# A hybrid attention and HGRN layer on one core: attention tails through one copy, six shared tiles for down sums, and the last channel's additions behind the meta rows

## The chip, the cores and the metric

The kernel runs on one core of a Trainium2 chip. The metric is the device time of one execution in microseconds. A core has TensorE (PE, matmuls; PEld is its weight load), VectorE (DVE), ScalarE (ACT), GpSimd (POOL) and SyncE (SP), which here issues the DMAs. Each engine runs its own queue in order and waits on semaphores of the others. Matmuls write PSUM, which has banks of 128 partitions by 512 float32; ACT and DVE read it.

## The reference

One layer over 16 meta rows and 1024 tokens (1040 rows, width 1024):

```python
a = rmsnorm(h, ln_mix_pre)
dq, dk, dv, hq, hf, hi, hg = split(a @ w_in)
y_diff = diff_attention(dq, dk, dv, ...)     # 4 heads, softmax minus lam * softmax, then rmsnorm
y_hgrn = hgrn2(hq, hf, hi, hg, ...)          # 4 heads, gated linear recurrence, rmsnorm * silu(g)
mix = concatenate([y_diff, y_hgrn]) @ w_out
h = h + rmsnorm(mix, ln_mix_post)
a = rmsnorm(h, ln_ffn_pre)
u = causal_conv3(a @ w_ffn_up) + conv_b      # 2 * 2816 channels
h = h + rmsnorm((gelu(gate) * up) @ w_ffn_down, ln_ffn_post)
return h[:, 16:, :]
```

All of it is float32. Products are made of three matmuls each: an operand is split into a rounded part `hi` and a remainder `lo`, and hi·hi, hi·lo and lo·hi are added.

## The kernel before, in words

The rows are taken in nine blocks: block 0 holds the meta rows (of which two are needed after the mixing), blocks 1 to 8 the 128-row blocks of tokens. The work on TensorE runs in four stretches:

- up to about 540 us, for each head the projections (`dense`), into which `interleave` puts the steps of attention (`attn`) and of the recurrence (`hgrn_head`) at set distances;
- 540 to 604 us, the first half of the output projection (`out_first`: columns 0 to 511, the first seven of eight channels of 128, into `y0`), with `hgrn_head` of head 3 between;
- 604 to 690 us, the second half, a loop over the blocks: matmuls into `py`, then `post` (norm, residual, norm, giving `a2`, in the profile `a`) and, some blocks later, `trans` (transposes of `a2`, copied to `at2`). The eighth channel comes last, since hgrn head 3 gives it: `out_last` adds it to `y0` from a bank `pz`, with the weight kept from the first half, and chunk 7 of block 1 waits for it likewise;
- then the up-projection with its convolution to about 1110 us, and the down-projection.

TensorE runs in the order in which the code is written. The other engines are ordered by the framework's scheduler, save where `issue_after` or `keep_in_program_order` hold an instruction back, and each engine's queue is then fixed. Tiles come from pools with a given number of buffers; who takes a buffer waits until its last reader is done.

In PSUM there are two banks with tag "ip" (projections, `py` of the first half, `pz`), two with tag "m" (`ss`, `pn`, `pt`, `pa`, `pl`) and two double ones with tag "S" (scores, `py` of the second half).

The tail of a piece of attention (`normed` with no gate; in a profile `ona`, `ss`, `msa`): the normed rows `on` are transposed into a bank `ss`; ACT multiplies the bank by the gain into the rounded `hi`, and DVE reads the bank again for the remainder `lo`. `to_nat` (`pn_vh`: values of the recurrence, transposed) takes the next "m" bank.

`down_sums` makes differences of down weights in spare time of stage one: four `wd` tiles are loaded, DVE subtracts, SP stores. `load_wo(n)` loads the eight output weights of half n through three raw tiles (`wor`) and splits them (`woh`, `wol`); `prep_plain` splits four up weights (`ra` into `uh`, `ul`). `halve` are POOL products over the forget gates in `hgrn_head`.

In the profile L53 is the wrapper through which most ACT and DVE instructions are issued, L146 the POOL subtraction of `split`, L336 the transposes of `to_nat`, L439 those products of `hgrn_head` that are called `pl`, L936 to L940 the three matmuls of `out_part`, and L1122 the transposes of `trans`.

Of the kernel before, what the change touches and what calls it, by code (L numbers as in the profile page):

```python
# [9 lines left out]
F32 = mybir.dt.float32  # L10
# [7 lines left out]
P = 128  # L18
# [4 lines left out]
KD = D // P  # L23
# [62 lines left out]
def layer_kernel(ctx: ExitStack, tc: tile.TileContext, x, meta, table, lbl, gpre, gpost, win,  # L86
# [54 lines left out]
    def ps_s(name):  # L141
        return pp.tile([P, 2, 512], F32, tag="S", name=name)

    def split(hi, lo, raw, eng=None):
        A.copy(hi, raw)
        (eng or G).tensor_tensor(lo, raw, hi.bitcast(F32), op=ALU.subtract)  # L146
# [21 lines left out]
    def parts_store(k, b0, b1, m, off):  # L168
        n = b1 - b0
        for l in range(2):  # L170
            SY.dma_start(msc[b0:b1, :, l, P * k:P * k + P].rearrange("b p c -> p b c"),
                         m[:, l, off:off + P * n].bitcast(F32).rearrange("p (b c) -> p b c", c=P))

    at_cm, atp = pool("at", 1)
    ahi = atp.tile([P, KD, L], F32R, tag="ahi", name="ahi")
    alo = atp.tile([P, KD, L], F32R, tag="alo", name="alo")
    ws_cm, wsp = pool("wdsums", 4)

    last_load = []

# [165 lines left out]

    late = []
    carry = []

    def carried():  # L350
        tails = list(carry)
# [40 lines left out]
    def hgrn_head(t, done=None):  # L392
# [9 lines left out]

        def halve(src, dst):
            pr = src.rearrange("p (b two) -> p b two", two=2)
            G.tensor_tensor(dst, pr[:, :, 0], pr[:, :, 1], op=ALU.mult)

        halve(f, t1)
        halve(t1, t2)
# [131 lines left out]
    def normed(k, b0, src, on, ss, C, n, gain, nm, raw=None, gate=None):  # L540
        if gate is None:
            V.scalar_tensor_tensor(ss[:C, :n], ss[:C, :n], 1.0 / 128, ss[:C, 4:4 + n], ALU.mult, ALU.add)
            A.activation(ss[:C, :n], ss[:C, :n], AF.Ln)
            A.activation(ss[:C, :n], ss[:C, :n], AF.Exp, scale=-0.5)
        else:
            rstd_of(ss[:C, :n], ss[:C, :n], 128.0)
        V.tensor_tensor(on[:C, :n], src, ss[:C, :n].rearrange("p (n o) -> p n o", o=1).to_broadcast([C, n, P]), op=ALU.mult)
        yield 1
        pt = ps_m(f"ss{nm}")
        W = start(b0 + n - 1) + rows(b0 + n - 1) - start(b0)  # L550
        for c in range(n):
            o = max(W - (n - c) * C, 0)
            T.transpose(pt[:, o:o + C], on[:C, c], ident[:C, :C])
        if gate is not None:
            V.scalar_tensor_tensor(raw, pt[:, :W], gain, gate, ALU.mult, ALU.mult)

        def halves(hi, lo, cols):
            if gate is None:
                A.mul(hi, pt[:, cols], gain)
                V.scalar_tensor_tensor(lo, pt[:, cols], gain, hi.bitcast(F32), ALU.mult, ALU.subtract)  # L560
            else:
                A.copy(hi, raw[:, cols])
                V.tensor_tensor(lo, raw[:, cols], hi.bitcast(F32), op=ALU.subtract)

        if b0 == 0:
            halves(m0[:, 0, k], m0[:, 1, k], slice(META - 2, META))
        first = max(b0, 1)
        if b0 + n > first:
            w = P * (b0 + n - first)
            m = parts_tile(nm)  # L570
            halves(m[:, 0, :w], m[:, 1, :w], slice(W - w, W))
            parts_store(k, first, b0 + n, m, 0)
        yield 1
# [327 lines left out]
            t_a, tiles_a = attn_in(h + 1)  # L901
            interleave(dense(tiles_a, None, wd_sums), [hgrn_head(t_h)] + carried(), FH, 1500)

    close(ws_cm, at_cm)
    wo_cm, wop = pool("wo", 10)
    y_cm, yp = pool("y0", 1)
    ml_cm, mlp = pool("mixload", 1)
    y0 = yp.tile([P, NBLK, 512], F32, tag="y0", name="y0")
    ssy = yp.tile([P, NBLK, 4], F32, tag="ssy", name="ssy")
    gpo0 = yp.tile([P, 512], F32, tag="gpo0", name="gpo0")  # L910
    SY.dma_start(gpo0, gpost[:, :512].to_broadcast([P, 512]))

    def load_wo(n):
        res = []
        for k in range(KD):
            raw = wp.tile([P, 512], F32, tag="wr", name=f"wor{n}_{k}", bufs=3)
            last_load.append(SY.dma_start(raw, wout[P * k: P * (k + 1), 512 * n: 512 * (n + 1)]))
# [49 lines left out]
    first_load(2)  # L967
    wo0 = load_wo(0)
    wo0_loaded = last_load[-1]

    def y0_gain(p):
        r = tok(p)[0]
# [2 lines left out]
    def out_last(p):  # L975
        r = tok(p)[0]
        py = ps_in(f"pz{p}")
        m = m0[:, :, KD - 1:] if p == 0 else m7[:, p - 1:p].rearrange("p b l t -> p l b t")
# [56 lines left out]
    def prep(q):  # L1035
        ft, j = divmod(q, 7)
        if ft >= NF or q in made:
            return
        if j == 0:
            load_raw4(ft)  # L1040
            src = raws["11"]
            w_sum("1", raws["21"], raws["22"], ALU.add)
        elif j == 1:
            src = w_sum("2", sums["1"], raws["11"], ALU.subtract)
        elif j == 2:
            src = sums["1"]
# [12 lines left out]
        made[q] = (hi, lo)  # L1059
# [3 lines left out]
    def prep_plain():  # L1063
        load_raw4(0)
        for j, nm in enumerate(("11", "12", "21", "22")):
            where = swp if j % 2 else wp
            hi = where.tile([P, 512], F32R, tag="wh", name=f"uh{nm}", bufs=4)
            lo = where.tile([P, 512], F32R, tag="wl", name=f"ul{nm}", bufs=4)
            split(hi, lo, raws[nm], G)
            plain[nm] = (hi, lo)  # L1070

    m7 = ep.tile([P, 8, 2, P], F32R, tag="e1", name="m7")
    for i in range(1, NBLK):
        SY.dma_start(m7[:, i - 1].bitcast(F32), msc[i][:, :, P * (KD - 1):])
    prep_plain()
    prep(7)
    wo = load_wo(1)
    gpo = qp.tile([P, 512], F32, tag="gpo", name="gpo", bufs=1)
    SY.dma_start(gpo, gpost[:, 512:].to_broadcast([P, 512]))
    gfb = qp.tile([P, D], F32, tag="gfb", name="gfb", bufs=1)  # L1080
# [78 lines left out]
        V.tensor_tensor(b21, b21, b22, op=ALU.subtract)  # L1159
        t_split(p, 5, b21, *last)  # L1160

    for i in (1, 0, 2, 3, 4, 5, 6, 7, 8):
        py = ps_s(f"py1_{i}")
        if i >= 3:
            y0_gain(i)
        if i == 0:
            for _ in out_part(m0, py[:, 0], wo, range(KD), True, True):
                pass
            post(i, py)
            continue  # L1170
        py = py[:, 0]
        m = blocks[i]
        if i + 1 < NBLK:
            second_load(i + 1)
        for _ in out_part(m, py, wo, range(4), True, False):
            pass
        if i == 3:
            trans(1)
            trans(0)
        if i > 3:  # L1180
            trans(i - 2)
        for _ in out_part(m, py, wo, range(4, 7 if i == 1 else 8), False, i > 1):
            pass
        if i == 1:
            for p in range(3):
                out_last(p)
            for _ in out_part(m7[:, 0:1].rearrange("p b l t -> p l b t"), py, wo[KD - 1:], range(1), False, True):
                pass
# [7 lines left out]
        if i < 4:  # L1196
            for p in (1 + 2 * i, 2 + 2 * i):
                out_last(p)
    close(q_cm, ml_cm, y_cm, wo_cm)

    xu_cm, xup = pool("xu", 2)
    t_cm, tp = pool("tsplit", 1)
# [365 lines left out]
```

## Time and profile before

| | us |
|---|---|
| median of 3 timed runs | 1354.03 (1353.2 to 1354.85) |
| profiled execution | 1361.32 |
| its span | 1359.5 |
| TensorE busy | 1296.5 |
| VectorE busy | 914.2 |
| ScalarE busy | 685.4 |
| GpSimd busy | 425.5 |

The mean granted clock of TensorE is 0.992. The span is what the profile covers, and the profiled execution is longer than the timed ones. In the rows of a timeline the first two numbers are start and duration in us, then engine, line, operation, what is written and read, and in brackets how long the engine had been idle before and who released it.

### The profile page before, as it was taken

The numbers are of one execution on the slowest core, as the hardware profiler recorded it, in microseconds if no ns is written. First come the engines' busy times: TensorE is split into PE (matmuls) and PEld (weight loads), VectorE is DVE, ScalarE is ACT, GpSimd is POOL, SyncE is SP. The second block draws the span as 40 slices with busy tenths as digits, with TensorE's granted clock in tenths as the row PEclk, the third lists the DMA queues.
The fourth block names the chain that finished last, engine by engine and source line by source line (L and its number), as shares of the span: only waits on it lengthen the run. The fifth ranks groups of instructions, "written<-read, shape, count | busy, mean of one in ns | idle before, by whom it ended". The sixth has DMA issues, their size and how long they took to land.

```text
span 1359.5 us, 26142 instructions
## 1 busy us (share of the span) xinstructions
PE 1296.5 (95%) x10170; PEld 1192.4 (88%) x10170; DVE 914.2 (67%) x1535; ACT 685.4 (50%) x1615; POOL 425.5 (31%) x334
## 2 busy tenths in 40 slices
PE   6999999999999998998998999999999999999997
PEld 5898989889989997675898999999999998888875
DVE  7666647564746464535698867877877776697586
ACT  6365346535644565335674444544554453554454
POOL 3211211021102110315127566566666641010021
PEclk9999999999999999998999999999999999999999
DMA  6332334243411221765612322223222225965363
GB/s 212 112 125 71 114 107 150 63 138 102 139 47 45 86 71 47 260 192 211 225 43 90 96 76 79 86 75 107 93 70 83 82 78 174 340 200 163 93 201 116
DMA packets 99570, 165.26 MB, mean 122 GB/s; under 512 B 10051, under 2 KB 34915, under 8 KB 99446
## 3 DMA queue, kind: packets, MB, share of 16 engines
q1 hardware_dynamic: 99446, 163.58, 36.6%
q8 instruction: 80, 1.31, 0.4%
q14 instruction: 44, 0.36, 0.1%
HBM read 122.91 MB, written 40.63 MB: 120 GB/s over the span
## 4 chain that ended last, share of the span: by engine, by line
PE 70%; DVE 11%; DMA 7%; ACT 6%; issue 4%; POOL 2%; SPq 1%; DVEq 0%; ACTq 0%; POOLq 0%
PE pd L1414 5%; PE pd L1415 5%; PE pd L1413 5%; PE pb L1255 4%; PE pb L1256 4%; PE pb L1257 4%; DMA wd<-in_wdown_dram 3%; PE pc L1255 2%; PE pa L1255 2%; PE pc L1257 2%; PE pa L1257 2%; PE pa L1256 2%; PE pc L1256 2%; PE pa L708 2%; DVE ast L53 2%
## 5 line engine op out<-in xcount | busy, mean ns | idle before, releaser
L1255 PE MATMUL pb<-t,uh 128*128 128x258 f32 x504 | 143.8, 285 | 5.8 <-DVE u L53 5.7
L1256 PE MATMUL pb<-t,uh 128*128 128x258 f32 x504 | 142.6, 283 | 0.0
L1257 PE MATMUL pb<-t,ul 128*128 128x258 f32 x504 | 142.3, 282 | 0.0
L1414 PE MATMUL pd<-wl,gh 128*128 128x512 f32 x308 | 121.9, 396 | 0.1
L1413 PE MATMUL pd<-wh,gh 128*128 128x512 f32 x308 | 121.7, 395 | 0.0
L1415 PE MATMUL pd<-wh,gl 128*128 128x512 f32 x308 | 121.7, 395 | 0.0
L53 DVE SCALAR_TENSOR_TENSOR c<-uu,cwt,c 128x514 f32<-128x514 f32 (+1 forms) x88 | 96.8, 1100 | 20.6 <-ACT c L53 19.9
L1255 PEld LDWEIGHTS pb<-t,uh 128*128 128x128 f32 x504 | 96.1, 191 | 7.1 <-DVE u L53 7.0
L1222 POOL TENSOR_TENSOR c<-c,c 128x514 f32<-128x514 f32 (+1 forms) x44 | 63.4, 1441 | 121.9 <-ACT c L53 119.2
L1256 PEld LDWEIGHTS pb<-t,uh 128*128 128x128 f32 x504 | 96.1, 191 | 0.0
L1257 PEld LDWEIGHTS pb<-t,ul 128*128 128x128 f32 x504 | 95.9, 190 | 0.0
L1255 PE MATMUL pa<-t,uh 128*128 128x258 f32 (+1 forms) x336 | 95.3, 283 | 0.0
L1256 PE MATMUL pa<-t,uh 128*128 128x258 f32 (+1 forms) x336 | 95.1, 283 | 0.0
L1257 PE MATMUL pa<-t,ul 128*128 128x258 f32 (+1 forms) x336 | 95.0, 283 | 0.0
L1255 PE MATMUL pc<-t,uh 128*128 128x258 f32 (+1 forms) x336 | 94.0, 280 | 0.0
L1257 PE MATMUL pc<-t,ul 128*128 128x258 f32 (+1 forms) x336 | 93.9, 280 | 0.0
L1256 PE MATMUL pc<-t,uh 128*128 128x258 f32 (+1 forms) x336 | 93.7, 279 | 0.0
L53 DVE SCALAR_TENSOR_TENSOR c<-ug,cwt,c 128x514 f32<-128x514 f32 (+1 forms) x88 | 86.0, 977 | 2.7 <-ACT c L53 2.0
L146 POOL TENSOR_TENSOR ul<-ws,uh 128x512 fp32r<-128x512 f32 x42 | 61.4, 1463 | 42.8 <-ACT uh L53 38.2
L1414 PEld LDWEIGHTS pd<-wl,gh 128*128 128x128 f32 x308 | 57.7, 187 | 15.1 <-DVE wl L53 0.9
L53 ACT ACTIVATE pb<-S,ast 128x528 f32<-128x528 f32 (+7 forms) x72 | 46.6, 649 | 47.1 <-DVE ast L53 47.0
L1413 PEld LDWEIGHTS pd<-wh,gh 128*128 128x128 f32 x308 | 57.7, 187 | 14.1
(348 smaller groups left out, 4144.7 us busy)
## 6 DMA issues: line engine op xcount, KB each, us to landing
ra<-in_wup_dram SPq DMA_DIRECT2D x88, 256.0 KB, 2.7
mp<-msc SPq DMA_DIRECT2D x23, 512.0 KB, 5.5
wd<-in_wdown_dram SPq DMA_DIRECT2D x44, 256.0 KB, 4.3
tsc<-wd SPq DMA_DIRECT2D x44, 256.0 KB, 2.6
wi<-tsc SPq DMA_DIRECT2D x44, 256.0 KB, 2.8
gi<-gsc SPq DMA_DIRECT2D x33, 256.0 KB, 4.5
wi<-in_wdown_dram SPq DMA_DIRECT2D x33, 256.0 KB, 2.9
gsc<-c SPq DMA_DIRECT2D x22, 257.0 KB, 2.2
```

The source lines that it names most:

```text
L53: ins = call(*args, **kw)
L146: (eng or G).tensor_tensor(lo, raw, hi.bitcast(F32), op=ALU.subtract)
L708: T.matmul(po[:, :P], w_, vn[:, j], start=(j == 0), stop=(j == i))
L1222: G.tensor_tensor(cg, cg, cu, op=ALU.mult)
L1255: T.matmul(pt, hi[:, s], th[:, k], start=(first and k == 0), stop=False, skip_group_check=True)
L1256: T.matmul(pt, hi[:, s], tl[:, k], start=False, stop=False, skip_group_check=True)
L1257: T.matmul(pt, lo[:, s], th[:, k], start=False, stop=(k == 3), skip_group_check=True)
L1413: T.matmul(py, gh[:, s], wh, start=(k == 0 and pr not in (3, 7)), stop=False, skip_group_check=True)
L1414: T.matmul(py, gh[:, s], wl, start=False, stop=False, skip_group_check=True)
L1415: T.matmul(py, gl[:, s], wh, start=False, stop=(k == NH - 1), skip_group_check=True)
```

## The change

1. Tails of attention: ACT's multiplication by the gain goes into `on` in SBUF and is the only read of the bank. Then ACT casts `hi` from there and DVE subtracts `lo` from there: one ACT instruction more for each piece, as many on DVE.
2. The pool of `wd` tiles has six instead of four, and stays open to the end of the second half. Its tiles then hold output weights 2, 3 and 4 of the first half and 6 and 7 of the second; the pool `wo` shrinks from ten to seven.
3. The POOL subtractions of the four plain up weights and of the second half's even output weights are issued after the last `halve` of hgrn head 3.
4. `gpo0` is loaded after the output weights; the plain up weights and the second half's output weights are called for ahead of the loads of channel 8 (`m7`).
5. In the second half the meta rows are taken inside block 1's turn, ahead of the last channel; `post(1)`, `post(0)` and `out_last(3)`, `out_last(4)` follow. `trans(0)` moves from block 3's turn to block 4's.

```diff
-    def split(hi, lo, raw, eng=None):
+    def split(hi, lo, raw, eng=None, after=None):
         A.copy(hi, raw)
-        (eng or G).tensor_tensor(lo, raw, hi.bitcast(F32), op=ALU.subtract)
+        with nullcontext() if after is None else tc.issue_after(after.ins):
+            (eng or G).tensor_tensor(lo, raw, hi.bitcast(F32), op=ALU.subtract)
...
+    ws_cm, wsp = pool("wdsums", 6)
     at_cm, atp = pool("at", 1)
...
-    ws_cm, wsp = pool("wdsums", 4)
...
-        if gate is not None:
+        if gate is None:
+            raw = on.rearrange("p n c -> p (n c)")[:, :W]
+            A.mul(raw, pt[:, :W], gain)
+        else:
             V.scalar_tensor_tensor(raw, pt[:, :W], gain, gate, ALU.mult, ALU.mult)

         def halves(hi, lo, cols):
-            if gate is None:
-                A.mul(hi, pt[:, cols], gain)
-                V.scalar_tensor_tensor(lo, pt[:, cols], gain, hi.bitcast(F32), ALU.mult, ALU.subtract)
-            else:
-                A.copy(hi, raw[:, cols])
-                V.tensor_tensor(lo, raw[:, cols], hi.bitcast(F32), op=ALU.subtract)
+            A.copy(hi, raw[:, cols])
+            V.tensor_tensor(lo, raw[:, cols], hi.bitcast(F32), op=ALU.subtract)
...
-    close(ws_cm, at_cm)
-    wo_cm, wop = pool("wo", 10)
+    close(at_cm)
+    wo_cm, wop = pool("wo", 7)
...
+            elif k < 5 if n == 0 else k > 5:
+                hi, lo = (wsp.tile([P, 512], F32R, tag="wd", name=f"wo{x}{n}_{k}") for x in "hl")
...
-            split(hi, lo, raw, V if k % 2 or (n == 0 and k) else G)
+            if k % 2 or (n == 0 and k):
+                split(hi, lo, raw, V)
+            else:
+                split(hi, lo, raw, G, halved[0] if n else None)
...
-            split(hi, lo, raws[nm], G)
+            split(hi, lo, raws[nm], G, halved[0])
...
-    for i in (1, 0, 2, 3, 4, 5, 6, 7, 8):
-        py = ps_s(f"py1_{i}")
...
+    for i in range(1, NBLK):
+        py = ps_s(f"py1_{i}")[:, 0]
...
         if i == 3:
             trans(1)
+        if i == 4:
             trans(0)
...
         if i == 1:
+            pm = ps_s("py1_0")
+            run(m0, pm[:, 0], wo, range(KD), True, True)
             for p in range(3):
                 out_last(p)
-            for _ in out_part(m7[:, 0:1].rearrange("p b l t -> p l b t"), py, wo[KD - 1:], range(1), False, True):
-                pass
+            run(k7(1), py, wo[KD - 1:], range(1), False, True)
+            post(1, py)
+            post(0, pm)
+            for p in (3, 4):
+                out_last(p)
+            continue
         post(i, py)
```

How this moves instructions, at three places. TensorE in the second half, at the end of the last channel's additions (`pz3` is the bank of `out_last(3)`, `py1_0` that of the meta rows, `py1_2` that of block 2). Before:

```order
L936 MATMUL pz3_7219<-woh0_7_6394,m7_7049 128x512
L938 MATMUL pz3_7219<-wol0_7_6395,m7_7049 128x512
L940 MATMUL pz3_7219<-woh0_7_6394,m7_7049 128x512
L936 MATMUL pz4_7227<-woh0_7_6394,m7_7049 128x512
L938 MATMUL pz4_7227<-wol0_7_6395,m7_7049 128x512
L940 MATMUL pz4_7227<-woh0_7_6394,m7_7049 128x512
L936 MATMUL py1_0_7235<-woh1_0_7098,m0_86 2x512
L938 MATMUL py1_0_7235<-wol1_0_7099,m0_86 2x512
```

and now:

```order
L941 MATMUL pz3_7259<-woh0_7_6407,m7_7136 128x512
L943 MATMUL pz3_7259<-wol0_7_6408,m7_7136 128x512
L945 MATMUL pz3_7259<-woh0_7_6407,m7_7136 128x512
L941 MATMUL pz4_7267<-woh0_7_6407,m7_7136 128x512
L943 MATMUL pz4_7267<-wol0_7_6408,m7_7136 128x512
L945 MATMUL pz4_7267<-woh0_7_6407,m7_7136 128x512
L941 MATMUL py1_2_7275<-woh1_0_7090,mp1_2_7150 128x512
L943 MATMUL py1_2_7275<-wol1_0_7091,mp1_2_7150 128x512
```

The 24 meta matmuls stood between `pz4` and block 2; they now stand ahead of `pz0`.

DVE in the second half, around `a2` of block 3 (`t0_0` and `t0_4` are the first split tiles for the up-projection). Before:

```order
L53 TENSOR_TENSOR tmp3_7390<-py1_3_7334,gpo_7144 128x512
L53 SCALAR_TENSOR_TENSOR xh3_7387<-y0_6340,ssy_6341,xh3_7387 128x512
L53 SCALAR_TENSOR_TENSOR xh3_7387<-tmp3_7390,ssy_6341,xh3_7387 128x512
L53 TENSOR_TENSOR y0_6340<-y0_6340,pz7_7403 128x512
L53 TENSOR_TENSOR y0_6340<-y0_6340,pz8_7411 128x512
L53 SCALAR_TENSOR_TENSOR a2_3_7389<-xh3_7387,ssy_6341,gfb_7146 128x1024
L53 TENSOR_TENSOR t0_0_7533<-at2_0_7045,t0_0_7533 128x1032
```

and now:

```order
L53 TENSOR_TENSOR tmp3_7379<-py1_3_7335,gpo_7145 128x512
L53 TENSOR_TENSOR y0_6354<-y0_6354,pz7_7392 128x512
L53 TENSOR_TENSOR y0_6354<-y0_6354,pz8_7400 128x512
L53 SCALAR_TENSOR_TENSOR xh3_7376<-y0_6354,ssy_6355,xh3_7376 128x512
L53 SCALAR_TENSOR_TENSOR xh3_7376<-tmp3_7379,ssy_6355,xh3_7376 128x512
L53 TENSOR_TENSOR t0_0_7534<-at2_0_7060,t0_0_7534 128x1032
L53 TENSOR_TENSOR t0_4_7537<-at2_0_7060,t0_4_7537 128x1032
L53 SCALAR_TENSOR_TENSOR a2_3_7378<-xh3_7376,ssy_6355,gfb_7147 128x1024
```

Two subtractions of split tiles have moved ahead of `a2` of block 3.

ACT in the attention of head 3, where its sixth block's exponentials stand (`pb3_6`). Before:

```order
L53 COPY ona3_3_5868<-pa3_4_5944 128x128
L53 COPY az1_117<-pt3_5_0_5978 16x128
L53 ACTIVATE pb3_6_5928,ast3_6_5929<-S3_6_1_5961,ast3_6_5929 128x784
L53 COPY ht3_0_5989<-pi_hi3_0_5926 128x272
L53 COPY at3_5_1_5994<-pt3_5_1_5993 128x256
L53 COPY vn3_5501<-pn_vh3_0_6016 16x128
```

and now:

```order
L53 COPY ona3_3_5882<-pa3_4_5958 128x128
L53 CAST woh0_2_6377<-wor0_2_6375 128x512
L53 COPY az1_117<-pt3_5_0_5992 16x128
L53 COPY ht3_0_6003<-pi_hi3_0_5940 128x272
L53 COPY at3_5_1_6008<-pt3_5_1_6007 128x256
L53 ACTIVATE pb3_6_5942,ast3_6_5943<-S3_6_1_5975,ast3_6_5943 128x784
L53 CAST woh0_3_6383<-wor0_3_6381 128x512
L53 COPY vn3_5513<-pn_vh3_0_6030 16x128
```

Casts of output weights, which wait for their loads, now stand between the steps of attention; before, those of weights 2 to 4 stood after it, beside the last gate.

More of the change, by code (lines that the diff above doesn't have):

```diff
@@ L348, in layer_kernel @@
     carry = []
+    halved = [None]
     def carried():
@@ L404, in halve @@
             pr = src.rearrange("p (b two) -> p b two", two=2)
-            G.tensor_tensor(dst, pr[:, :, 0], pr[:, :, 1], op=ALU.mult)
+            halved[0] = G.tensor_tensor(dst, pr[:, :, 0], pr[:, :, 1], op=ALU.mult)
         halve(f, t1)
@@ L910, in layer_kernel @@
     gpo0 = yp.tile([P, 512], F32, tag="gpo0", name="gpo0")
-    SY.dma_start(gpo0, gpost[:, :512].to_broadcast([P, 512]))
     def load_wo(n):
@@ L969, in layer_kernel @@
     wo0_loaded = last_load[-1]
+    SY.dma_start(gpo0, gpost[:, :512].to_broadcast([P, 512]))
     def y0_gain(p):
@@ L977, in out_last @@
         py = ps_in(f"pz{p}")
-        m = m0[:, :, KD - 1:] if p == 0 else m7[:, p - 1:p].rearrange("p b l t -> p l b t")
+        m = m0[:, :, KD - 1:] if p == 0 else k7(p)
         for _ in out_part(m, py, wo0[KD - 1:], range(1), True, True):
@@ L1068, in prep_plain @@
             lo = where.tile([P, 512], F32R, tag="wl", name=f"ul{nm}", bufs=4)
-            split(hi, lo, raws[nm], G)
+            split(hi, lo, raws[nm], G, halved[0])
             plain[nm] = (hi, lo)
+    prep_plain()
+    wo = load_wo(1)
     m7 = ep.tile([P, 8, 2, P], F32R, tag="e1", name="m7")
@@ L1074, in layer_kernel @@
         SY.dma_start(m7[:, i - 1].bitcast(F32), msc[i][:, :, P * (KD - 1):])
-    prep_plain()
-    prep(7)
-    wo = load_wo(1)
     gpo = qp.tile([P, 512], F32, tag="gpo", name="gpo", bufs=1)
@@ L1160, in t_sums, with run, k7 @@
         t_split(p, 5, b21, *last)
-    for i in (1, 0, 2, 3, 4, 5, 6, 7, 8):
-        py = ps_s(f"py1_{i}")
+    def run(*args):
+        for _ in out_part(*args):
+            pass
+    def k7(i):
+        return m7[:, i - 1:i].rearrange("p b l t -> p l b t")
+    for i in range(1, NBLK):
+        py = ps_s(f"py1_{i}")[:, 0]
         if i >= 3:
             y0_gain(i)
-        if i == 0:
-            for _ in out_part(m0, py[:, 0], wo, range(KD), True, True):
-                pass
[L1169 to L1172, printed above, removed]
         if i + 1 < NBLK:
             second_load(i + 1)
-        for _ in out_part(m, py, wo, range(4), True, False):
-            pass
+        run(blocks[i], py, wo, range(4), True, False)
         if i == 3:
             trans(1)
+        if i == 4:
             trans(0)
@@ L1181, in layer_kernel @@
             trans(i - 2)
-        for _ in out_part(m, py, wo, range(4, 7 if i == 1 else 8), False, i > 1):
-            pass
+        run(blocks[i], py, wo, range(4, 7 if i == 1 else 8), False, i > 1)
         if i == 1:
+            pm = ps_s("py1_0")
+            run(m0, pm[:, 0], wo, range(KD), True, True)
             for p in range(3):
                 out_last(p)
-            for _ in out_part(m7[:, 0:1].rearrange("p b l t -> p l b t"), py, wo[KD - 1:], range(1), False, True):
-                pass
+            run(k7(1), py, wo[KD - 1:], range(1), False, True)
[4 more added lines that the diff above has]
+            continue
         post(i, py)
@@ L1195, in layer_kernel @@
             t_split(0, 6, quarter(0, 6), mxp, "X1", WN[0])
-        if i < 4:
+        if i in (2, 3):
             for p in (1 + 2 * i, 2 + 2 * i):
                 out_last(p)
-    close(q_cm, ml_cm, y_cm, wo_cm)
+    close(q_cm, ml_cm, y_cm, wo_cm, ws_cm)
     xu_cm, xup = pool("xu", 2)
```

## The prediction

> **What bounds the kernel now.** I read the page first, then the list of what TensorE waited for, then the timeline around its longest waits.
>
> ```profile
> PE 1296.5 (95%) x10170; PEld 1192.4 (88%) x10170; DVE 914.2 (67%) x1535; ACT 685.4 (50%) x1615; POOL 425.5 (31%) x334
> ...
> PE pn_vh L336 <- DVE msa L53: 5.0, 3, 1.7
> PE pl L439 <- DVE hq L53: 3.6, 3, 1.6
> PE pa L1122 <- ACT at L53: 3.3, 2, 3.0
> PE pa L708 <- ACT pb L53: 2.8, 6, 0.8
> PE pz L936 <- DVE y L53: 2.2, 1, 2.2
> PE py L938 <- POOL wol L146: 0.9, 1, 0.9
> PE pa L708 <- DVE msa L53: 0.9, 1, 0.9
> PE py L936 <- ACT woh L53: 0.7, 1, 0.7
> ```
>
> TensorE works 95% of the span and runs a fixed order, so a change that leaves its instructions alone can only win what it waits, and what it runs slowly after a wait. The first line is the page's; the others give total us, number of waits and the longest. These are the waits at the edited places; the sum over them is the stock.
>
> **Tails of attention.** Three of the waits stand in heads 1 to 3. Head 1, on the timeline:
>
> ```profile
> 250.98 0.49 PE L553 MATMUL ssa<-ident,ona 128*128 128x128 f32 x3
> 251.51 0.58 ACT L53 ACTIVATE msa<-ssa,sub 128x384 fp32r<-128x384 f32 x1 [1.06 <-PE ssa L553]
> ...
> 252.81 0.61 DVE L53 SCALAR_TENSOR_TENSOR msa<-ssa,sub,msa 128x384 fp32r<-128x384 f32 x1
> 253.47 0.55 PE L336 MATMUL pn_vh<-ident,ht 128*128 128x128 f32 x3 [1.65 <-DVE msa L53]
> 253.52 0.70 ACT L53 ACTIVATE pb<-S,ast 128x528 f32<-128x528 f32 x1 [1.43 <-DVE ast L53]
> ...
> 254.87 0.48 ACT L53 COPY vn<-pn_vh 128x384 f32<-128x384 f32 x1
> 255.03 0.75 PE L708 MATMUL pa<-avn,az 128*128 128x128 f32 x2 [0.31 <-ACT pb L53]
> ```
>
> `pn_vh` needs the PSUM bank of `ssa`, and the DVE subtraction that frees it ends at 253.42 because reductions for the next scores run ahead of it. Afterwards ScalarE's multiplication, which ends at 252.09, frees it: 1.3 us earlier. The added cast costs ScalarE 0.58 us as the multiplication does, and it fits into the 1.43 us that ScalarE then sits idle; without that idle time it would stand in front of the exponentials. The other casts (a small one and two more in each head) I cost at nothing for the same reason, the 1.06 idle before the multiplication; uncovered they would be 4 x 1.3 = 5 us on ScalarE. The `vn` copy moves ahead of them too, so the 0.31 of `pa` may go. I take 1.3 for each of heads 1 and 2. In head 0 the only such wait is the 0.86 of `pa` (the 0.9 above); I take 0.3.
>
> Head 3 is worse off. Casts of output weights 2, 3 and 4 now stand in ScalarE's queue inside its attention, each behind a load, and each next load waits for the subtraction of the one before (one raw buffer goes round):
>
> ```profile
> 494.79 4.00 SPq L917 DMA_DIRECT2D wor<-in_wout_dram  x2
> ...
> 501.75 0.26 ACT L53 COPY az<-pt 16x128 f32<-16x128 f32 x1 [1.46 <-PE pt L684]
> 505.08 0.52 ACT L53 COPY vn<-pn_vh 16x128 f32<-16x128 f32 x2 [1.49 <-PE pn_vh L336]
> ...
> DMA to landing us min/median/max: 2.7/3.4/6.4
> ```
>
> The last row is of all 16 loads of output weights. Weight 2's is the second of the two issues that end at 498.8. With landings of 2.9, a cast of 0.6 and a subtraction of about 1, the casts end at about 502, 507 and 512, so exponentials that began between 502 and 510 come 1 to 2 us late. What follows them on TensorE was not waiting, so most is slack; I leave head 3 a gain of 0.7. Tails together: 1.3 + 1.3 + 0.7 + 0.3 = 3.6. Bounds: 5.9 (all of the 5.0 and the 0.9 go), and -1 (gain nothing, exponentials of head 3 late beyond slack).
>
> **Six tiles for down sums.** DVE runs in order, and one subtraction that waits for its load holds up the hgrn products behind it:
>
> ```profile
> 297.55 0.71 DVE L53 TENSOR_TENSOR wd<-wd,wd 128x512 f32<-128x512 f32 x1 [1.36 <-DMA wd<-in_wdown_dram]
> 300.71 0.48 PE L439 MATMUL pl<-hq,kr 128*32 128x16 f32 x36 [1.32 <-DVE hq L53]
> ```
>
> Two more tiles let loads be issued earlier. Of 1.32 I take 0.6; bounds 2.1 (with the other short `pl` wait, 3.6 - 1.3 - 1.6 = 0.7) and -0.5, since one projection load now stands behind two more of these on SP's queue.
>
> **Last tail of head 3, first half of the output projection.**
>
> ```profile
> 539.92 0.33 SPq L911 DMA_DIRECT2D gpo<-in_gpost_dram  x1
> ...
> 551.07 0.62 ACT L53 CAST uh<-ra 128x512 fp32r<-128x512 f32 x1 [2.46 <-DMA ra<-in_wup_dram]
> 553.55 0.62 DVE L53 SCALAR_TENSOR_TENSOR msa<-ssa,sub,msa 128x384 fp32r<-128x384 f32 x1 [2.67 <-ACT msa L53]
> 554.90 1.76 DVE L53 TENSOR_TENSOR hq<-hq,f 128x520 f32<-128x520 f32 x1
> 556.81 0.69 PE L439 MATMUL pl<-hq,kr 128*32 128x16 f32 x62 [1.56 <-DVE hq L53]
> ```
>
> The subtraction stands ahead of `hq` on DVE and waits 2.67 for a ScalarE that sits behind casts of loads. In the new order the up-weight loads stand ahead of the gain's load (`gpo`, which holds SP until 539.9) instead of behind it, and three output weights follow; the subtraction should come 0.8 to 1.3 us earlier, and the POOL subtractions that slowed `hq` (they now follow the halving of `f`) no longer run beside it. I take 1.3 of the 1.56, bounds 1.56 and -0.5. The load issued earlier has a price where the gate is computed; that is a rival below.
>
> **Meta rows first, last channel after them.** Everything between the first matmul of block 1 and the first of block 2 in the second half:
>
> ```profile
> 604.75 0.39 PE L936 MATMUL py<-woh,mp 128*128 128x512 f32 x1
> ...
> 615.51 0.51 PE L936 MATMUL pz<-woh,m 128*128 128x512 f32 x1 [2.24 <-DVE y L53]
> ...
> 617.07 0.63 PE L936 MATMUL pz<-woh,m 128*128 128x512 f32 x1
> ...
> 625.50 0.39 PE L936 MATMUL py<-woh,mp 128*128 128x512 f32 x1
> ...
> 619.87 0.69 DVE L53 TENSOR_TENSOR y<-y,pz 128x512 f32<-128x512 f32 x1 [0.59 <-PE pz L940]
> 620.47 0.68 DVE L53 TENSOR_TENSOR tmp<-py,gpo 128x512 f32<-128x512 f32 x1
> 615.00:620.00 5.00, 4.49 (x13) 3.13 (x14) 3.07 (x6) 4.38 (x15) 4.71 (x4) 0.69 0.62 235
> 640.00:645.00 5.00, 5.00 (x17) 4.00 (x18) 0.15 (x1) 0.20 (x3) 1.28 (x1) 0.66 0.62 210
> ```
>
> That is 20.75 us for 63 matmuls. Undisturbed ones start 0.2325 us apart (604.75 on), 14.65 in all; the rest is the waits for weights 6 and 7 (0.7 and 0.9), the 2.24, and the matmuls after 617.07, which run 0.63 instead of 0.39 and start 0.43 apart: seven of them, 1.4 us. The last two rows are 5-us slices; the next to last three numbers begin with the granted clock, 0.69 and 0.66 after waits of 2.24 and 3.02.
>
> Now 24 meta matmuls (5.6 us) stand before the last channel. They cover the late weights (seventh and eighth are needed 5 us later) and the DVE work that held `y`. New: the third `pz` needs the bank of the first, read by an addition of 0.69, perhaps 0.25 us late; and block 2 needs the bank of block 1, freed by `tmp`, which stands behind the additions of `pz` 3 and 4. After the last `pz` that is one addition and `tmp`, 0.69 + 0.68 and two handovers: 1.55. In before, 24 matmuls lay between. Sum: 14.65 + 0.25 + 1.55 + 0.4 for starts = 16.85, a gain of 3.9. Bounds: 5.8 (no new wait) and 1.8 (2.5 us for `tmp`, and then the slow stretch of 1.4 again).
>
> **Transposes of the meta rows one block later.**
>
> ```profile
> 639.33 0.41 PE L1122 MATMUL pa<-ident,xh 2*128 2x2 f32 x4 [3.02 <-ACT at L53]
> ...
> 650.02 1.95 DVE L53 SCALAR_TENSOR_TENSOR a<-xh,ssy,gfb 128x1024 f32<-128x1024 f32 x1 [1.10 <-ACT ssy L53]
> 652.72 2.65 DVE L53 TENSOR_TENSOR t<-at,t 128x1032 fp32r<-128x1032 f32 x2 [0.75 <-ACT t L53]
> 655.45 1.03 PE L1122 MATMUL pa<-ident,a 128*128 128x128 f32 x8
> ...
> 669.92 0.75 DVE L53 SCALAR_TENSOR_TENSOR xh<-y,ssy,xh 128x512 f32<-128x512 f32 x1 [2.82 <-DMA xh<-in_x_dram]
> ```
>
> They waited 3.0 + 0.3 for copies out of the banks, and the slow stretch after them costs 1.4: 4.7 goes; a block of matmuls (5.6 us) later the banks are free, so 0.4 comes back at most. Late next: `a` of block 3. It now stands behind the two `t` subtractions (2.65) on DVE and ends 26.4 us after block 2's start, while TensorE, 4.7 us quicker, wants it at 25.2: a new wait of 1.2 (0 to 3, then with the slow stretch). The `xh` load of block 4 waits for the moved transposes and is issued some 3 us later relative to TensorE; at a landing of 4 to 8 us it still just makes it. Net 4.7 - 0.4 - 1.2 = 3.1, less 0.2 for blocks 5 to 8: 2.9. Bounds 4.7 and -0.3.
>
> On the clock the Trainium skill ("TensorE: Matmul & The Clock Gate", Part 1) says it drops to half after an idle window of about 3.4 us, on a free-running clock, and needs as long a busy one to return. By that rule waits of 2.24 and 3.02 need cost nothing but themselves, and a new one of 1.55 nothing more; the trace has 0.69 and 0.66 after such waits, so it bears the rule out only if the window counts a mostly idle stretch.
>
> **Sum.** 3.6 + 0.6 + 1.3 + 3.9 + 2.9 = 12.3 us. It is made on the profiled execution, 1361.3 with a span of 1359.5, so that comes to 1349.0; the median of the timed runs, 1354.03, stands 7.3 lower, and I carry the difference over: 1341.7. All bounds together, 20.1 and -0.5, give 1334 and 1354.5. After 690 the orders are alike and TensorE is nearly full, so the shift should reach the end. The new `gpo0` place and the later POOL subtractions cost nothing: POOL is 31% busy, and its next consumers come after 570.
>
> **Rivals.**
> 1. New waits eat the gain between 604 and 660: `tmp` 2.5 us late and `a` of block 3 3 us late, each with 1.4 of slow matmuls. Those two terms then give 1.8 - 0.3 instead of 6.8: 12.3 - 5.3 = 7.0, time 1347. For it: DVE runs in order, and both stand behind work for others. Against: it idles 0.59, 0.75 and 1.10 there in the rows above.
> 2. The tails give next to nothing, because TensorE then waits for the exponentials (the 2.8 us, six times) instead of the bank. 12.3 - 3.2 = 9.1: 1345. Against: 0.31 each in these places.
> 3. The slow matmuls are not the waits' doing and stay, 1.4 twice: 12.3 - 2.8 = 9.5: 1344.5. This is where the clock rule above leads.
> 4. DVE's chain after 672 (split tiles, `xh` loads such as the 2.82 at 669.92) sets when the up-projection can begin, not TensorE's arrival. Then only 1 or 2 us survive: 1353.
> 5. Slower: ScalarE held by casts that wait for loads. At the longest landing seen, 6.4 instead of 2.9, the three in head 3 add 3 x 3.5 = 10.5, less about 3 us of slack; the same before the gate (two up-weight casts now ahead of it) adds 3.5; each with 1.4 slow. 7.5 + 1.4 + 3.5 + 1.4 = 13.8 lost against 12.3: 1355.5, and beyond 1356.7 when each landing passes about 6.8. Against: the median is 3.4.
>
> **How the numbers follow.** Forecast 0.52 (1341.7, own range 1338 to 1345), rivals in order 0.15, 0.11, 0.07, 0.07, 0.08. A measurement tells 0.2% apart, 2.7 us: faster is below 1351.3, slower above 1356.7. The forecast and rivals 1 to 3 are faster (0.85, less 0.01 for their tails), rival 4 and half of rival 5 the same (0.11), the rest slower (0.05). The range leaves out rivals 4 and 5 and a little at the fast end: 1336 to 1351.5.
>
> **What would show it.** `pn_vh` waits for ScalarE's multiplication, under 0.4 us, in heads 1 to 3; no `py` wait for `woh` or `wol`; from block 1's to block 2's start about 16.9; `py` of block 2 waits for `tmp`; the meta transposes wait under 0.5; those of block 3 wait for `a`; granted clock 1.00 in the slices where 0.69 and 0.66 stood. It is wrong if ScalarE in head 3 waits for `wor` by more than 3 us at a time with TensorE idle behind it, or if the first up-projection matmul does not come 10 to 12 us earlier.

## The result and the profile after

| | median us | runs | ratio to before, 95% interval |
|---|---|---|---|
| before, beside the first runs | 1354.44 | 4 | |
| changed, first runs | 1344.92 (1340.98 to 1345.7) | 4 | 0.9925 [0.9904, 0.9946] |
| changed, second time | 1343.26 (1342.07 to 1348.69) | 6 | 0.9909 [0.9884, 0.9933] |
| changed, third time | 1346.10 (1344.26 to 1348.14) | 6 | 0.9910 [0.9882, 0.9937] |

One further execution of before, of 3216.56 us in the second comparison, is in the slow state and counts in no ratio.

The change saves 9.5 us in the first comparison and about 12 by the ratio of the two later ones; 12.3 was forecast, 1341.7. The first profile of the changed kernel has a span of 1343.9, in an execution of 1345.7. That is 15.6 less than the profiled execution of before, more than any of the ratios give. The first experiment returns to this.

The page's first line and the list of TensorE's waits, after:

```profile
PE 1290.4 (96%) x10170; PEld 1189.0 (88%) x10170; DVE 910.7 (68%) x1535; ACT 690.6 (51%) x1631; POOL 429.7 (32%) x334
...
PE pl L441 <- DVE hq L53: 5.3, 4, 1.8
...
PE py L941 <- DVE gate L53: 2.4, 1, 2.4
...
PE pl L435 <- DVE hq L53: 2.1, 2, 1.2
PE pa L709 <- ACT pb L53: 1.9, 3, 0.8
...
PE pa L1127 <- DVE a L53: 1.4, 1, 1.4
PE py L941 <- DVE tmp L53: 1.4, 1, 1.4
...
PE pn_vh L337 <- ACT pb L53: 1.2, 1, 1.2
PE pn_vh L337 <- ACT ona L53: 1.0, 3, 0.3
...
PE pa L1127 <- ACT at L53: 0.2, 1, 0.2
```

The 5.0 of `pn_vh` in heads 1 to 3 is 1.0 (the 1.2 is in head 0), the waits for `pz`, `woh` and `wol` are gone, and the 3.3 at the transposes of the meta rows is 0.2. New are the two of 1.4, for `tmp` and for `a`. Both were named. Not named were the 2.1 at L435 (which waits for the products `hq` of levels 5 and 6 of the recurrence) and the gate's 2.4 instead of 1.9. L441 grew from 3.6 to 5.3.

The tail of head 1, after, on the timeline:

```profile
249.38 0.58 ACT L53 ACTIVATE ona<-ssa,sub 128x384 f32<-128x384 f32 x1 [0.99 <-PE ssa L555]
249.99 0.52 ACT L53 CAST msa<-ona 128x384 fp32r<-128x384 f32 x1
250.59 0.48 ACT L53 COPY vn<-pn_vh 128x384 f32<-128x384 f32 x1
...
251.52 0.69 ACT L53 ACTIVATE pb<-S,ast 128x528 f32<-128x528 f32 x1
...
250.01 0.55 PE L337 MATMUL pn_vh<-ident,ht 128*128 128x128 f32 x3 [0.32 <-ACT ona L53]
...
251.13 0.49 PE L709 MATMUL pa<-avn,az 128*128 128x128 f32 x2
```

`pn_vh` starts 0.05 us after the multiplication ends. The cast, the `vn` copy and a weight cast fill the time in which ScalarE used to wait for the maxima, and the exponentials begin only 0.15 after the last maximum's end (251.37). `pa`, which waited 0.31, waits for nothing.

The stretches of the program in the first profiles, from the starts of the same matmuls (the gate's, block 1's first, block 2's first, and the one of the up-projection that waits for `ug`, at 690.38 before and 674.74 after; the first of the up-projection come 11 us ahead of it, between the last blocks), and in a second profile of each:

| from ... to | before | after | before again | after again |
|---|---|---|---|---|
| start ... gate | 543.4 | 535.4 | 543.5 | 533.5 |
| gate ... block 1 | 61.4 | 62.1 | 61.9 | 62.4 |
| block 1 ... block 2 | 20.8 | 16.5 | 20.9 | 16.5 |
| block 2 ... up-projection | 64.9 | 60.7 | 62.4 | 59.5 |
| up-projection ... end of span | 669.1 | 669.2 | 666.4 | 669.1 |

### The profile page after: what moved, and what is told of

The parts are those of the page before. It is cut to its first block, busy times and chain, and to the rows that moved or that the text cites. A ratio compares the mean times of both kernels' runs of the same rounds, so it can differ in the third digit from the quotient of the medians.

```text
span 1343.9 us, 26160 instructions
## 1 busy us (share of the span) xinstructions
PE 1290.4 (96%) x10170; PEld 1189.0 (88%) x10170; DVE 910.7 (68%) x1535; ACT 690.6 (51%) x1631; POOL 429.7 (32%) x334
## 3 DMA queue, kind: packets, MB, share of 16 engines
q8 instruction: 80, 1.31, 0.4%
## 4 chain that ended last, share of the span: by engine, by line
PE 47%; DVE 5%; DMA 3%; ACT 3%; issue 3%; POOL 2%; SPq 0%; DVEq 0%; ACTq 0%; POOLq 0%
PE pd L1424 5%; PE pd L1423 5%; PE pd L1425 5%; PE pb L1265 4%; PE pb L1266 4%; PE pb L1267 4%; PE pc L1265 2%; PE pa L1265 2%; PE pc L1267 2%; PE pa L1267 2%; PE pa L1266 2%; PE pc L1266 2%; PE py L945 1%; PE py L941 1%; PE py L943 1%
## 5 line engine op out<-in xcount | busy, mean ns | idle before, releaser
L1425 PEld LDWEIGHTS pd<-wh,gl 128*128 128x128 f32 x308 | 57.7, 187 | 14.1
```

The costliest lines, as they stand in the source:

```text
L1425: T.matmul(py, gl[:, s], wh, start=False, stop=(k == NH - 1), skip_group_check=True)
```

## The experiments

**Before and after once more.** Both kernels unchanged, five rounds, with second profiles.

> The kernel before, unchanged, timed against itself and profiled a second time. Theory: its first profiled execution (1361.3) held five stretches of 3.4 us at half clock (near 68, 256, 618, 641 and 788 us) of which each costs 1.7 us, and whether a wait of 1.6 to 3 us starts such a stretch is chance; this profile then shows the same waits within 0.1 us, another set of stretches, and a time nearer 1354. Rival: the stretches belong to the waits; then the same five come back and the profiled time is again about 1361. Either way the ratio of the timed runs is 1.000, within 0.001.

> The changed kernel, unchanged, for a narrower interval and a second profile. Theory (gain 9.5 us in the timed runs, spread by 0 to 3 half-clock stretches): ratio 0.993, interval inside 0.991 to 0.995; waits as in its first profile, stretches elsewhere. Rival (the first profile's difference, 15.6 us, is the true one): ratio 0.9885.

Before against itself gave 1.0008 [0.9989, 1.0028], its profiled execution 1356.87; after gave 0.9909, just outside the 0.991 to 0.995 that was expected. The single runs of before spread from 1349.3 to 1363.6. Over 29 of them the time falls as the granted clock rises, from 0.988 to 0.996 (r squared, the share of the variance that goes with it, is 0.76). Where the clock is lost is seen in slices of 2.5 us. First the stretch near 256 in the first profile of before, then one after the gate in the first profile of after, then the place near 615 in the second profile of before (the third number from the end is the granted clock):

```profile
255.00:257.50 2.50, 2.47 (x12) 2.47 (x12) 0.32 (x2) 0.86 (x2) 1.26 (x1) 0.52 0.02 7
```

```profile
537.50:540.00 2.50, 2.50 (x8) 1.95 (x7) 0.00 (x0) 1.11 (x2) 0.00 (x0) 0.53 0.72 269
```

```profile
612.50:615.00 2.50, 2.50 (x8) 1.16 (x5) 0.68 (x2) 0.62 (x1) 2.42 (x3) 0.59 1.02 368
615.00:617.50 2.50, 1.34 (x4) 1.11 (x4) 2.34 (x4) 1.91 (x5) 2.21 (x3) 0.50 1.02 383
617.50:620.00 2.50, 2.50 (x7) 1.90 (x7) 0.69 (x1) 1.99 (x7) 2.50 (x3) 0.54 0.38 146
```

Summed over slices of 1 us, each stretch is 3.4 us at half clock, sometimes two in a row (6.8), so that 1.7 us of work is lost in each. Before had them at 67, 255, 617, 641 and 788 the first time, and at 183, 255, 545, 613 (double) and 640 the second. So neither theory holds as stated: three of five places came back, two did not. Over the fourteen profiles of this study, between 33 and 750 us: after waits of TensorE of 1.0 to 1.5 us a stretch followed in 3 of 96 cases, of 1.5 to 2 in 19 of 63, of 2 and more in 26 of 30.

What looks like chance within these odds is a grid. In each profile all stretches lie a whole number of steps of 3.413 us apart: the five of the first profile of before, which start at 67.38, 255.11, 616.92, 640.82 and 787.59, are 55, 106, 7 and 43 steps apart. Here are two pairs of neighbouring cells of that grid in this profile (length, time in which TensorE was busy, granted clock):

```profile
180.02:183.43 3.41, 1.74 (x14) 1.00 0.84 276
183.43:186.85 3.42, 2.36 (x17) 1.00 0.44 166
251.70:255.11 3.41, 1.45 (x9) 1.00 0.38 115
255.11:258.52 3.41, 3.41 (x16) 0.50 0.10 16
```

A wait of 2.73 us, up to 184.49, is cut by the border at 183.43, and no stretch follows. The 1.65 of `pn_vh`, up to 253.47, lies in one cell, and the next runs at half clock. In all fourteen profiles, between 33 and 750 us, 49 cells held 1.68 us or more of idle time on TensorE, about half a cell, and 48 of them were followed by a cell at half clock. Of the 2892 other cells 6 were: four are the first halves of double stretches, which stay unexplained, and in two the transposes of `trans` stand beside 1.3 us of idle time. The grid starts at another point in each execution, so the same wait is cut in one and whole in the next.

The first profile of before holds five stretches and that of after three, which is 3.4 of the 15.6 us between them; the 12.2 that remain agree with the later ratios. The stretches are not all that differs: the second profile of before has one more than the first, counting the double one as two, and is 4.5 us shorter.

**The tails alone, the loop alone.** For the first, only `normed` as changed; for the second, only the loop of the second half:

```diff
# e2_tails_only, on before
+        if gate is None:
+            raw = on.rearrange("p n c -> p (n c)")[:, :W]
+            A.mul(raw, pt[:, :W], gain)
...
# e3_half2_only, on before
-    for i in (1, 0, 2, 3, 4, 5, 6, 7, 8):
+    for i in range(1, NBLK):
...
+            run(m0, pm[:, 0], wo, range(KD), True, True)
```

> The kernel before with the tails' part of the change alone (one copy out of PSUM; four tiles for down sums, old second half). Theory: pn_vh waits 0.3 instead of 1.65 in heads 1 to 3, pa no longer 0.3 after it, about 1.8 us for each head, and 0 to 1 in head 0: 4 to 6 us faster, ratio 0.9956 to 0.997. Rival (the exponentials of ScalarE bind instead): 1.5 us or less, ratio 0.999.

> The kernel before with the new loop of the second half alone (meta rows ahead of the last channel, transposes of the meta rows a block later; tails, pools and POOL's order as before). Theory: the 20.75 us from block 1 to block 2 become 16.5 to 17.5, the 3.3 us of waits at the meta transposes go, new waits of about 1.4 for tmp and for a of block 3: 6 to 8.5 us faster, ratio 0.9937 to 0.9956. Rival (the new waits eat it, or the two late weights, loaded as before, still hold block 1): 3 us or less, ratio 0.998.

Tails alone: 0.9960 [0.9944, 0.9975], 5.4 us by the ratio. `pn_vh` waits 0.32 in all three heads and `pa` nothing, as the theory has it; rival 2 of the prediction falls. The loop alone: 0.9973 [0.9953, 0.9993], 3.7 us, where 6 to 8.5 was expected. Its wait list has why: its own new waits are as expected, but the late weights are still there, 2.5 us where before had 1.5:

```profile
612.69 0.50 PE L936 MATMUL py<-woh,mp 128*128 128x512 f32 x1 [1.67 <-ACT woh L53]
614.04 0.50 PE L938 MATMUL py<-wol,mp 128*128 128x512 f32 x1 [0.85 <-POOL wol L146]
...
626.17 0.50 PE L936 MATMUL py<-woh,mp 128*128 128x512 f32 x1 [1.38 <-DVE tmp L53]
```

Block 1 to block 2 takes 19.5 instead of 16.5. TensorE asks for this weight at the same place in both orders; why it waits longer here is not shown. The profile also has slow stretches, at 516 and 568, that belong to the old first half.

**The parts on weights, and all without them.** Six tiles, held-back POOL, order of loads, on before; then tails and loop together without these.

```diff
# e8_weights_only: the changed kernel with normed and the loop as before
# e8_tails_half2: before with normed and the loop as changed
```

> The kernel before with the second to fourth part of the change alone (six shared tiles, POOL's subtractions held back, order of the loads); tails and loop of the second half as before. Theory: the two waits for weights near 610 (1.6) go and come back in part as a longer wait for y; waits of 0.6, 1.2 and 1.0 at levels 4 to 6 and 0.5 at the gate come, that at level 2 (1.0 to 1.6) goes: no difference, ratio 0.998 to 1.002. Rival (the earlier weights carry 3 us, what e2 and e3 leave of the whole): ratio 0.9975.

> The kernel before with the tails' part and the new loop together, without the parts on weights. Theory (the parts on weights are worth nothing in the first half, and in the second save the 1.6 to 2.5 us of waits for weights 6 and 7): 8 to 11 us faster than before, ratio 0.992 to 0.994, 1 to 3 us slower than the changed kernel beside it. Rival (they cost as much in the first half as they save): equal to the changed kernel.

Weights alone: 0.9996 [0.9978, 1.0014], nothing. The weights do come in time, and all of it is handed to the next wait, for `y`, which was 2.24 before:

```profile
616.29 0.80 PE L942 MATMUL pz<-woh,m 128*128 128x512 f32 x1 [4.65 <-DVE y L53]
```

Without them: 0.9919 [0.9888, 0.9950], against 0.9910 for the changed kernel beside it, which the intervals do not tell apart. In its profile block 1 to block 2 takes 20.9, with 1.43 and 0.86 for the weights and a slow stretch; the 16.5 needs both parts. What the weights save there they cost elsewhere: gate to block 1 is 64.6 in the weights' kernel, with two slow stretches (3.4) in it, and 61.4 or 61.9 in before, with none and one.

**POOL's subtractions.** The next two put them elsewhere: not held back at all, or on VectorE behind the last level.

```diff
# e4_not_held, on the changed kernel
-            split(hi, lo, raws[nm], G, halved[0])
+            split(hi, lo, raws[nm], G)
...
# e5_dve_behind_levels, on the changed kernel (levels[0]: the last copy into am)
-            split(hi, lo, raws[nm], G, halved[0])
+            split(hi, lo, raws[nm], V, levels[0])
```

(In both, output weights 0 and 2 of the second half go the same way.)

> The changed kernel without its third part: POOL's subtractions of the plain up weights and of the second half's even output weights are no longer held behind the last halving. Theory (held back, they run beside the products of levels 4 to 6, which then take 1.3 to 1.8 us instead of 0.7 and make TensorE wait 0.6, 1.2 and 1.0): those three waits shrink to under 0.4 together, a wait of 1.0 to 1.6 comes back at level 2; 0 to 2 us faster than the changed kernel, ratio to before 0.988 to 0.992. Rival (holding them back is what makes the first half faster, as the prediction has it): 1 to 2 us slower than the changed kernel.

> The changed kernel with those subtractions (four plain up weights, output weights 0 and 2 of the second half) on VectorE behind the last level instead of on POOL behind the last halving. Theory: with POOL idle the products of levels 3 to 6 take 0.7 and the waits of 0.6, 1.2 and 1.0 go: 2 to 3 us faster than the changed kernel, ratio to before 0.987 to 0.990. Rival (the products are slow for another reason): the waits stay, no faster.

The changed kernel first, then the second of these, at the same products of the recurrence:

```profile
553.62 6.84 POOL L147 TENSOR_TENSOR ul<-ra,uh 128x512 fp32r<-128x512 f32 x4
560.43 3.00 POOL L147 TENSOR_TENSOR wol<-wor,woh 128x512 fp32r<-128x512 f32 x2
...
562.20 1.78 DVE L53 TENSOR_TENSOR hq<-hq,tt 128x512 f32<-128x512 f32 x1
...
564.13 0.70 PE L435 MATMUL pl<-hq,kr 128*32 128x32 f32 x32 [1.19 <-DVE hq L53]
```

```profile
554.77 1.19 POOL L407 TENSOR_TENSOR tt<-tt 128x65 f32<-128x65 f32 x4
596.99 1.31 POOL L147 TENSOR_TENSOR wol<-wor,woh 128x512 fp32r<-128x512 f32 x1 [41.03 <-DMA m<-msc]
...
564.14 0.68 DVE L53 TENSOR_TENSOR hq<-hq,tt 128x512 f32<-128x512 f32 x1
```

With POOL silent the same product takes 0.68 instead of 1.78 and no level waits over 0.4. Gate to block 1 falls from 62.1 to 62.4 in the changed kernel to 60.4, and the ratio to before is 0.9871 [0.9856, 0.9887]. Not held back: the three waits at later levels go as well, none comes back at level 2, gate to block 1 is 60.7, ratio 0.9891 [0.9874, 0.9908]. So holding them back moved the collision from the product ahead of level 2 to the products of levels 4 to 6, and cost 1.3 to 1.6 us there, or 2.6 to 2.9 with the slow stretches taken off (a double one follows the gate here); the timed runs, whose intervals overlap with the changed kernel's, do not show this size. The rival falls.

**Order in the second half.**

```diff
# e6_second_half, on the changed kernel
-            for p in (3, 4):
-                out_last(p)
+            with tc.issue_after(tmps[1].ins):
+                for p in (3, 4):
+                    out_last(p)
...
+            with tc.issue_after(a2s[3].ins):
+                t_split(0, 0, quarter(0, 0), ep, "e0")
+                t_split(0, 4, quarter(0, 4), ep, "e1")
```

> The changed kernel with two orders on VectorE set in the second half: tmp of block 1 ahead of the additions of pz 3 and 4, and a of block 3 ahead of the first two split tiles. Theory (both waits are order alone): the 1.4 at block 2 (for tmp) goes to 0.2 or less, the 0.8 to 1.4 at the transposes of block 3 to 0.3 or less: 1.8 to 2.5 us faster than the changed kernel. Rival (xh's load and ScalarE's squares bind the chain of a): the second stays above 0.8, 1.3 us faster.

This failed: 0.9917 [0.9902, 0.9932]. In its profile:

```profile
616.13 0.69 DVE L53 TENSOR_TENSOR tmp<-py,gpo 128x512 f32<-128x512 f32 x1 [1.83 <-ACT junk L53]
...
616.87 0.50 PE L941 MATMUL py<-woh,mp 128*128 128x512 f32 x1 [1.24 <-DVE tmp L53]
...
626.45 0.51 PE L941 MATMUL py<-woh,mp 128*128 128x512 f32 x1 [2.35 <-DVE tmp L53]
```

VectorE, put first, only waits: ScalarE's square of the same bank comes ahead of `tmp` and stands in ScalarE's queue behind the squares of `y`. The wait at block 2 stays 1.24, and the additions pushed back delay block 3 by 2.35, with a slow stretch after it. The wait for `a` of block 3, 0.80, is as in the second profile of the changed kernel (0.82). My theory that order on VectorE alone makes these waits is wrong. What would take them away stays open; a bank that is free sooner was not tried.

**Together, and the version that is kept.** All of the last edits, with the up weights' casts behind the gate on ScalarE; then the same without the order in the second half.

```diff
# e7_all = e5 + e6 + this; e8_best = e5 + this
+            with tc.issue_after(gated[0].ins):
+                split(hi, lo, raws[nm], V, levels[0])
```

> The two before together, and the casts of the plain up weights behind the last gate on ScalarE. Theory: the wait for the gate goes from 2.4 to 1.9, sums add up: 4 to 6 us faster than the changed kernel, ratio to before 0.986 to 0.989, and fewer slow stretches after 530. Rival (the casts then hold up the last tail): the tail's multiplication comes later and level 2 waits over 1 us.

> The changed kernel once more, beside the next three on the same chip. In ten profiles so far 19 of 21 waits of TensorE of 2 us or more were followed by one 3.4 us stretch at half clock, 12 of 44 between 1.5 and 2, and 1 of 72 between 1.0 and 1.5. Theory: this profile has a stretch after the wait near 180 (2.5 to 3) and after that for the gate (2.4 or more), and none after pn_vh. Ratio to before 0.990 to 0.993.

> The changed kernel with the subtractions on VectorE behind the last level and the plain up weights' casts behind the last gate (the second half as the change has it). Theory: waits at levels 3 to 6 under 0.5 together, gate 1.9, 1.4 for tmp and 0.8 to 1.4 for a as in the changed kernel: 3 to 4 us faster than the changed kernel beside it, ratio to before 0.987 to 0.989. Rival (the first half's gain is given back at 600 by later weights): 1 us or less.

The first gave 0.9880 [0.9864, 0.9896], with the two waits for `tmp` (1.22 and 1.27) as in e6; the gate waits 1.92 as expected, and the last tail is not late. The changed kernel beside the second had the two slow stretches that were expected, near 184 and after the gate, none after `pn_vh`, and two more, at 68 and 290. The second gave 0.9876 [0.9848, 0.9904], median 1341.5 beside 1346.1 for the changed kernel. Its waits from 530 to 700 us are these four and no others above 0.2:

```profile
PE py L942 <- DVE gate L53: 1.9, 1, 1.9
PE pq L1248 <- ACT ug L53: 1.6, 1, 1.6
PE py L942 <- DVE tmp L53: 1.4, 1, 1.4
PE pa L1129 <- ACT at L53: 1.3, 1, 1.3
```

It is faster than both kernels by median, 4.6 us over the changed one: its six runs lie from 1339.5 to 1344.5, those of the changed kernel from 1344.3 to 1348.1, though the intervals of the two ratios overlap. The cast's share of the time is not shown, since without it the ratio was 0.9871. Its effect on the gate's wait is: 1.93 here and 1.92 in the first, against 2.48 without it and 2.40, 2.52 and 3.27 in the three profiles of the changed kernel.

## Why the prediction was right, step by step

**Tails, 3.6 forecast.** The mechanism is as described and the size too small: 1.65 in each of heads 1 to 3 (1.33 at `pn_vh`, 0.3 at `pa`), 5.0 together, and e2's 5.4 by time. The step that failed is the discount of head 3 to 0.7. Its casts of output weights do stand in ScalarE's queue, but the exponentials that came late were not on the path: what they cost TensorE there is 0.18 at one score matmul (another waits 0.24, for VectorE). ScalarE's longest wait there for such a load is 1.32, under the 3 that would have spoken for rival 5. Head 0 gave little; its wait moved to `pn_vh` (1.16, for ScalarE's exponentials).

**Six tiles, 0.6 forecast.** No gain is seen, and no run has this part alone. The wait of 1.32 near 300 is gone in the changed kernel, and there are 1.79 one level earlier and 1.18 two levels earlier, the latter behind a subtraction of `wd` tiles that still waits 1.09 for its load. For the 1.32 the prediction named only the load. First before, then after, ahead of the waits of 1.32 and 1.79:

```profile
298.23 1.77 POOL L146 TENSOR_TENSOR wl_dv<-wr_dv,wh_dv 128x512 fp32r<-128x512 f32 x1 [0.52 <-ACT wh_dv L53]
298.80 1.77 DVE L53 TENSOR_TENSOR hq<-hq,t 128x520 f32<-128x520 f32 x1
```

```profile
289.49 1.72 POOL L147 TENSOR_TENSOR wl_dv<-wr_dv,wh_dv 128x512 fp32r<-128x512 f32 x1 [12.52 <-ACT wh_dv L53]
290.00 1.76 DVE L53 TENSOR_TENSOR hq<-hq,tt 128x520 f32<-128x520 f32 x1
```

Both times `hq` starts beside POOL's subtraction of a projection weight and takes 1.8, where the product at 285.70 after takes 0.69 with POOL idle. This is the collision that e5 shows in head 3, and more tiles do not touch it.

**First half, 1.3 forecast: not gained.** The wait at level 2 went (1.56 and 0.96 before), but gate to block 1 got 0.5 to 0.7 longer. With 1.7 taken off for each slow stretch in it, it is 61.4 and 60.2 before and 60.4 to 60.7 in the three profiles of the changed kernel: no gain, and the longer time is the stretch. Two omissions: that the POOL work, moved behind the halving, would meet the products of levels 4 to 6 (waits of 0.5, 1.2 and 0.9, which e5 takes away); and the gate, which I had left to rival 5 alone. There the rival's mechanism was real and its size smaller than priced:

```profile
531.63 0.62 ACT L53 CAST uh<-ra 128x512 fp32r<-128x512 f32 x1 [1.57 <-DMA ra<-in_wup_dram]
...
535.44 0.50 PE L941 MATMUL py<-woh,mp 128*128 128x512 f32 x1 [2.40 <-DVE gate L53]
```

The cast waits 1.57 for its load ahead of the gate's first exponential; the gate's wait, 1.92 and 1.93 before, grows by 0.5 to 1.3 and crosses 2 us, where the slow stretch became all but sure (1.7 more).

**Meta rows first, 3.9 forecast (16.85).** 16.5 in all three profiles: 4.2 to 4.4. The new wait for `tmp` is 1.38 where 1.55 was worked out. One step was wrong all the same: that the meta rows cover both late weights. The two waits for weights before are both for the seventh, its rounded part and its remainder, in block 1's own matmuls:

```profile
609.78 0.50 PE L936 MATMUL py<-woh,mp 128*128 128x512 f32 x1 [0.67 <-ACT woh L53]
611.15 0.51 PE L938 MATMUL py<-wol,mp 128*128 128x512 f32 x1 [0.87 <-POOL wol L146]
```

Those stand ahead of the meta rows in the new order too, 18 matmuls after the block's first, so only the eighth is needed later. The loop alone and the tails with the loop still waited for the seventh (1.67 and 0.85, 1.43 and 0.86); what removed the wait is the part on weights. The term came out because both parts were in the change.

**Transposes a block later, 2.9 forecast.** 64.9 to 60.7 and 62.4 to 59.5, so 4.2 and 2.9. The wait for `a` is 1.44 and 0.82 against 1.2. The chain after it, rival 4, did not bind: the wait for `ug` at the up-projection is 1.31 and 0.74, and was 1.59 and 1.26.

**The slow matmuls, 1.4 each.** They are 1.7, and they do go with the waits, so rival 3 falls: after 615 and 640 the clock is 1.00 in every slice of the changed kernel between 600 and 645. The Trainium skill ("TensorE: Matmul & The Clock Gate", Part 1) has the length of the stretch, the half clock and a free-running window as seen here; an idle window of about 3.4 us does not fit, since about 1.7 us of idle time in a window was enough. The prediction's condition, a window that counts when it is mostly idle, is close to this. What it missed is that new waits run the same risk.

**The sum.** 12.3 forecast, 9.5 to 12 measured: larger tails by about 1.5 and the second half by 0.5 to 1.5, the first half by about 2 to 4 the other way, the slow stretch at the gate included. That the sum came out close is partly luck, since these errors have opposite signs. The first matmul of the up-projection comes 15.4 and 16.2 us earlier (679.13 to 663.76, 677.74 to 661.50), where 10 to 12 was to be the sign; with 1.7 taken off for each slow stretch ahead of it, 12.0 and 9.4. The sum's base, one profiled execution, held five stretches; subtracting from the median was right.

## What to carry to other kernels

When PSUM banks hold up TensorE, look which engine reads the bank last and why that engine is late; one quick read by an idle engine was worth 1.6 us a place here, and the extra instruction cost nothing that is seen, because it filled that engine's own wait. Work that is moved out of one collision lands beside something else: look what stands on the neighbouring engines for as long as it lasts. Price a wait of 2 us as nearly 4 in a kernel like this, and a wait of 1.4 as 1.4. Between these, whether 1.7 more is lost depends on where the wait falls on the clock's grid, and a single profile shows one throw of it.

## What the runs showed of the hardware

TensorE's slow stretches are quantised: 3.4 us at half clock, 1.7 us lost, sometimes twice in a row. In each of the fourteen profiles they lie on a grid of 3.413 us, and between 33 and 750 us a cell at half clock followed 48 of the 49 cells in which TensorE stood idle for 1.68 us or more, and 6 of the 2892 others. Seen by waits: after 26 of 30 of 2 us or more, 19 of 63 of 1.5 to 2, and 3 of 96 of 1.0 to 1.5. They go with much of the spread between executions of the same program (1349 to 1365 us for before; r squared 0.76 between time and granted clock in 29 of them). Two single profiles of before differ by 4.5 us where the timed medians agree.

A 128x512 product of two SBUF tiles on VectorE took 0.68 us with GpSimd silent and 1.78 beside GpSimd's subtractions of the same size.
